# A decoder layer on one core: another written order for the first two row tiles' steps

## The chip, the cores and the metric

The kernel runs on one core of a Trainium2 chip. The core has a matrix engine (TensorE, PE in the profile, with PEld for its weight loads), a vector engine (VectorE, DVE), a scalar engine (ScalarE, ACT), a general engine (GpSimd, POOL) and an engine that here only issues transfers (SyncE, SP). Each works through a queue of its own in the order in which its instructions were put there; semaphores make one engine wait for another. The metric is the time of one execution in device microseconds (us), as the median of several runs. Lower is better.

## The reference

One layer of a decoder trunk over 1024 tokens behind 16 learned meta tokens, width 1024, all in float32:

```python
h = concat([meta, x])
u = rmsnorm(h, mix_norm_pre)
q, f_logit, i_in, g_out, v_pool, gate_a, gate_b = split(u @ w_in)
a = hgrn2(q, f_logit, i_in, g_out, ...)         # gated linear recurrence, 4 heads
p = multiscale_pool(v_pool, pool_proj, pool_scale)
z = sigmoid(gate_a) * (a @ w_branch_hgrn) + sigmoid(gate_b) * (p @ w_branch_pool)
h = h + rmsnorm(z @ w_out, mix_norm_post)
u = rmsnorm(h, ffn_norm_pre)
y = (gelu(causal_dwconv(u @ ffn_w_gate)) * (u @ ffn_w_up)) @ ffn_w_down
h = h + rmsnorm(y, ffn_norm_post)
return h[16:]
```

The change lies in the first microseconds: the norm `u` of the first rows and the columns `i_in` of the first product, `v = u @ w_in[:, 1024:1536]`.

## The kernel before

A float32 product is made from three products of a rounded type. Each operand is cut into a high part (rounded) and a low part (the rest, what the rounding left): high by high, high by low, low by high. On the weights' side a pair is `whi` and `wlo`; on the rows' side it is `uhi` and `ulo`. The rounding is done by ACT, the rest (a subtraction) by DVE. `mm3` (line 188) makes the three products at lines 190, 191 and 192: by `uhi` with `whi`, `uhi` with `wlo`, and `ulo` with `whi`.

Row tiles have 128 tokens. `vtiles` (line 458) lists nine, the 16 meta rows among them. The features (1024) are eight blocks of 128, called k. A product needs the rows with the features on the partitions, so each row tile is scaled by its norm, transposed by PE in 128 x 128 blocks (four into one PSUM bank, `pt`), and read out of PSUM twice, by ACT for `uhi` and by DVE for `ulo`. The weights of `v` arrive in four loads of 512 KB (`wiraw`), each with two k.

For the first two row tiles (number 0 and 1 in `vtiles`) the steps are written out one by one in a stage in which the order of ACT, DVE and PE is that of the text (`manual_schedule`, line 1033). The transfers were all issued ahead of it, on SP: row tile 0, weights 0, row tile 1, weights 1 to 3, and then the other rows. The step functions are these, with i the row tile, j a half of the row or a load of weights, k a feature block:

- `warm(n)` (line 501): n products of constants into a bank that nobody reads, which keep PE working while nothing else is there.
- `pe.transpose(gp, grow, ...)` and `gcol` (lines 1036 to 1038): the norm's gains are transposed and copied by DVE, so that k's gains stand along the partitions.
- `sq(i)`: ACT squares and sums row tile i, ACT takes the root, DVE the reciprocal.
- `scaled(i, j)`: DVE scales half j of row tile i into `un`.
- `turn(i, j)`: four PE transposes into the bank `pts[i, j]`, which then holds k = 4j to 4j+3.
- `hi_(i, k)` and `lo_(i, k)`: ACT multiplies by the gain and rounds into `uhi`; DVE multiplies and subtracts into `ulo`. Both read the bank.
- `wi_hi(j, part)` and `wi_lo(j, part)`: the same cut for load j of the weights, in halves (`ha`, `hb`, one k each) or whole.
- `mm_(i, k)`: the three products of row tile i and block k, summed in the bank `vb[i]`.

Behind these steps come `v_norm(2)` and `v_norm(3)` (norms of the next rows, on ACT and DVE), `v_feat` (their transposes, line 424), and the products of the other seven row tiles. The same stage runs on to the gates' first products. In later stages only PE's order is written out, and a planner, which works with modelled times when the kernel is built, sets the order of ACT, DVE, POOL and SP. The late stages use Strassen's form for the big products (lines 310 to 313), and the last product, with `w_down`, runs at lines 190 to 192 again.

Of the kernel before, what the change touches and what calls it, by code (L numbers as in the profile page):

```python
# [19 lines left out]
KD = D // P  # L20
# [49 lines left out]
def trunk_kernel(ctx: ExitStack, tc: tile.TileContext, x, meta_tokens, mix_norm_pre,  # L70
# [4 lines left out]
    act, dve, pool_e, pe = nc.scalar, nc.vector, nc.gpsimd, nc.tensor  # L75
# [20 lines left out]
    def nm(s):  # L96
        cnt[0] += 1
        return f"{s}_{cnt[0]}"
# [7 lines left out]
    def bank(name="ps"):  # L106
        return stage["ps", "p"].tile([P, 512], F32, tag="ps", name=nm(name))
# [11 lines left out]
    def small(shape, name, tag, bufs=4):  # L119
        return sm.tile(shape, F32, tag=tag, name=nm(name), bufs=bufs)  # L120

    def rr(a):
        return a.bitcast(F32)
# [377 lines left out]
    def warm(n):  # L501
        for _ in range(n):
            pe.matmul(junk_bank[:, :P], onesm, ident, start=True, stop=True)
# [12 lines left out]
    def v_mm(ps, t0, k):  # L516
        hi, lo = wi[k // 2]
        c = slice((k % 2) * 512, (k % 2) * 512 + 512)
        if t0 == 0:
            for n, b_ in ((2 * NM, hi), (NM, lo))[:: -1 if k else 1]:  # L520
                pe.matmul(ps[:n], um[:, k, :n], b_[:, c], start=(k == 0 and n > NM), stop=(k == KD - 1),
                          skip_group_check=True)
            return
        mm3(ps[:, :], (uhi[:, k, t0 : t0 + P], ulo[:, k, t0 : t0 + P]), (hi[:, c], lo[:, c]), k == 0, k == KD - 1)
# [506 lines left out]
    vb = [bank("pv") for _ in range(2)]  # L1031
    E = mybir.EngineType
    with tc.manual_schedule(engines={E.Activation, E.DVE, E.PE}):
        warm(8)
        gp = bank("pp")
        pe.transpose(gp[:, :KD], grow[:KD], ident[:KD, :KD])
        gcol = small([P, KD], "gcol", "gcol")
        dve.tensor_copy(gcol, gp[:, :KD])
        warm(6)
        wi += [tuple(wst.tile([P, 1024], F32R, tag=t, name=nm(t)) for t in ("whi", "wlo")) for _ in range(3)]  # L1040
        wi.append((slot(1024, F32R, "wihi"), slot(1024, F32R, "wilo")))
        pts, un_, rs_ = {}, {}, {}
# [1 line left out]
        def wi_hi(j, part=slice(0, 1024)):  # L1044
            act.copy(wi[j][0][:, part], raws[j][:, part])

        def wi_lo(j, part=slice(0, 1024)):
            dve.tensor_tensor(wi[j][1][:, part], raws[j][:, part], rr(wi[j][0][:, part]), ALU.subtract)

        def sq(i):  # L1050
            ssq = small([P, 1], "ssq", "nq")
            un_[i] = slot(D, name="un")
            act.activation(un_[i], rows_in[i], AF.Square, accum_out=ssq)
            rs_[i] = row_rstd(ssq, P, "n")

        def scaled(i, j):
            n = slice(j * 512, (j + 1) * 512)
            dve.tensor_scalar(un_[i][:, n], rows_in[i][:, n], rs_[i], None, ALU.mult)

        def turn(i, j):  # L1060
            pts[i, j] = bank("pt")
            for n in range(4):
                pe.transpose(pts[i, j][:, n * P : (n + 1) * P], un_[i][:, (4 * j + n) * P : (4 * j + n + 1) * P], ident)

        def u_at(i, k):
            t0 = vtiles[i][0]
            return (pts[i, k // 4][:, (k % 4) * P : (k % 4 + 1) * P], uhi[:, k, t0 : t0 + P], ulo[:, k, t0 : t0 + P])

        def hi_(i, *ks):
            for k in ks:  # L1070
                src, hi, lo = u_at(i, k)
                act.activation(hi, src, AF.Copy, scale=gcol[:, k : k + 1])

        def lo_(i, *ks):
            for k in ks:
                src, hi, lo = u_at(i, k)
                dve.scalar_tensor_tensor(lo, src, gcol[:, k : k + 1], rr(hi), ALU.mult, ALU.subtract)

        def mm_(i, *ks):
            for k in ks:  # L1080
                v_mm(vb[i], vtiles[i][0], k)

        ha, hb = slice(0, 512), slice(512, 1024)
        sq(0)
        scaled(0, 0)
        wi_hi(0, ha)
        wi_lo(0, ha)
        turn(0, 0)
        hi_(0, 0)
        lo_(0, 0)  # L1090
        wi_hi(0, hb)
        wi_lo(0, hb)
        hi_(0, 1)
        lo_(0, 1)
        mm_(0, 0, 1)
        scaled(0, 1)
        turn(0, 1)
        sq(1)
        hi_(0, 2, 3)
        wi_hi(1)  # L1100
        scaled(1, 0)
        turn(1, 0)
        lo_(0, 2)
        wi_lo(1, ha)
        scaled(1, 1)
        lo_(0, 3)
        wi_lo(1, hb)
        hi_(1, 0, 1)
        lo_(1, 0, 1)
        mm_(0, 2)  # L1110
        mm_(1, 0, 1)
        turn(1, 1)
        mm_(0, 3)
        hi_(0, 4, 5)
        lo_(0, 4, 5)
        hi_(1, 2, 3)
        wi_hi(2)
        lo_(1, 2, 3)
        wi_lo(2)
        mm_(1, 2, 3)  # L1120
        mm_(0, 4, 5)
        hi_(0, 6, 7)
        lo_(0, 6, 7)
        hi_(1, 4, 5)
        wi_hi(3)
        lo_(1, 4, 5)
        mm_(1, 4, 5)
        wi_lo(3)
        hi_(1, 6, 7)
        lo_(1, 6, 7)  # L1130
# [761 lines left out]
```

## Time and profile before

| | us |
|---|---|
| median of 3 runs | 1309.5 (1308.31 to 1310.21) |
| profiled execution, its own time | 1310.05 |
| span of that execution in the profile | 1308.3 |
| PE without work in the span (1308.3 less 1291.9 busy) | 16.4 |
| first useful product of the two tiles starts | 9.48 |
| transposes behind their last product start | 24.31 |

Times of rows in the trace are us from the span's start. A row of the timeline gives start, duration, engine, line, operation, what is written from what, the shape, and how many like instructions were merged (x); in brackets stands the idle time of the engine ahead of it and what ended that. A row of the waits gives who waited for whom: total, times, longest. A row of the windows gives the stretch, its length, the busy time of PE, PEld, DVE, ACT and POOL with their instructions, the granted clock of PE, the share of the DMA engines and GB/s. A PE row's duration runs to the modelled end of a product; products overlap, and what counts is the distance of their starts.

### The profile page before, as it was taken

What the parts mean: (1) busy time and instruction counts of PE and PEld (TensorE: products, weight loads), DVE (VectorE), ACT (ScalarE), POOL (GpSimd) and SP (SyncE); (2) the same over time, 40 slices, a digit from 0 to 9 for tenths busy, and PEclk for the clock granted to TensorE, in tenths of its full rate; (3) what the DMA queues carried; (4) which work ended last, traced back from release to release, by engine and by line L of the source; (5) the groups of instructions that cost most, each with busy time, mean ns of one, the idle gap of its engine ahead of it and who ended that gap; (6) DMA issues with size and microseconds to landing.
All of it is one profiled execution on the core that took longest, in us unless ns stands there. A gap on an engine that the chain in (4) does not pass through costs nothing.

```text
span 1308.3 us, 21993 instructions
## 1 busy us (share of the span) xinstructions
PE 1291.9 (99%) x8651; PEld 1140.8 (87%) x8651; DVE 965.3 (74%) x1311; ACT 527.2 (40%) x918; POOL 356.1 (27%) x308
## 2 busy tenths in 40 slices
PE   8999999999999999999999999999999999999998
PEld 7799899999999899978898888888888888888887
DVE  6768965454776877765588999888898985455758
ACT  6554433332244546235563222322322232444443
POOL 3015333130000000150045655553755552000000
PEclk9999999999999999999999999999999999999999
DMA  8135542325524767776777787568777799666644
GB/s 277 42 106 164 194 158 102 122 89 153 170 67 144 231 236 238 281 224 242 242 257 249 192 222 176 172 181 207 167 180 169 154 247 294 209 225 226 227 173 161
DMA packets 143817, 247.62 MB, mean 189 GB/s; under 512 B 11008, under 2 KB 75180, under 8 KB 143714
## 3 DMA queue, kind: packets, MB, share of 16 engines
q1 hardware_dynamic: 127026, 213.42, 48.7%
q0 software_dynamic: 12064, 24.38, 11.3%
q10 hardware_dynamic: 4624, 8.41, 1.7%
q8 instruction: 68, 1.11, 0.4%
q14 instruction: 35, 0.29, 0.1%
HBM read 174.12 MB, written 95.09 MB: 206 GB/s over the span
## 4 chain that ended last, share of the span: by engine, by line
PE 95%; DVE 1%; ACT 1%; DMA 1%; issue 0%; POOL 0%; DVEq 0%; ACTq 0%; SPq 0%; POOLq 0%
PE P L310 17%; PE P L311 17%; PE P L313 17%; PE pd L190 5%; PE pd L191 5%; PE pd L192 5%; PE pm L190 2%; PE pm L192 2%; PE pm L191 2%; PE ppv L210 1%; PE ppv L214 1%; PE ppv L211 1%; PE pba L210 1%; PE pba L211 1%; PE pg L210 1%; PE pv L192 1%
## 5 line engine op out<-in xcount | busy, mean ns | idle before, releaser
L311 PE MATMUL P<-v,whi 128*128 128x512 f32 (+2 forms) x408 | 140.7, 353 | 0.0
L310 PE MATMUL P<-v,whi 128*128 128x512 f32 (+2 forms) x408 | 140.7, 352 | 0.0
L313 PE MATMUL P<-v,wlo 128*128 128x512 f32 (+2 forms) x424 | 135.1, 349 | 0.0
L281 POOL TENSOR_TENSOR swa<-wraw,wraw 128x512 f32<-128x512 f32 x32 | 48.9, 1530 | 188.0 <-DMA wraw<-in_w_in_dram 77.3
L255 ACT CAST whi<-wraw 128x512 fp32r<-128x512 f32 x90 | 53.1, 618 | 101.5 <-PE P L311 86.9
L1602 DVE TENSOR_TENSOR rot<-wraw,rot 128x1024 fp32r<-128x1024 f32 x31 | 38.0, 1225 | 72.2 <-ACT rot L1601 72.2
L310 PEld LDWEIGHTS P<-v,whi 128*128 128x128 f32 x408 | 76.7, 188 | 10.4
L311 PEld LDWEIGHTS P<-v,whi 128*128 128x128 f32 x408 | 76.6, 188 | 10.2
L313 PEld LDWEIGHTS P<-v,wlo 128*128 128x128 f32 x424 | 74.0, 188 | 10.8
L192 PE MATMUL pd<-rot 128*128 128x512 f32 x274 | 82.5, 388 | 0.0
L191 PE MATMUL pd<-rot 128*128 128x512 f32 x274 | 82.5, 388 | 0.0
L190 PE MATMUL pd<-rot 128*128 128x512 f32 x274 | 81.9, 388 | 0.1
L256 DVE TENSOR_TENSOR wlo<-wraw,whi 128x512 fp32r<-128x512 f32 x86 | 74.5, 889 | 2.7 <-ACT whi L255 2.7
L255 ACT CAST whi<-swa 128x512 fp32r<-128x512 f32 x64 | 38.2, 619 | 91.9 <-PE P L311 81.2
L256 DVE TENSOR_TENSOR wlo<-swb,whi 128x512 fp32r<-128x512 f32 x64 | 67.9, 1068 | 9.0 <-ACT whi L255 8.7
L1601 ACT CAST rot<-wraw 128x1024 fp32r<-128x1024 f32 x31 | 32.7, 1054 | 90.8 <-PE pd L192 89.4
L310 PE MATMUL P<-uhi,whi 128*128 128x258 f32 (+2 forms) x240 | 68.6, 303 | 0.0
L311 PE MATMUL P<-ulo,whi 128*128 128x258 f32 (+2 forms) x240 | 68.4, 303 | 0.0
L255 ACT CAST whi<-swb 128x512 fp32r<-128x512 f32 x64 | 38.1, 618 | 69.3 <-PE P L311 61.0
L310 PE MATMUL P<-t2h,whi 128*128 128x258 f32 (+2 forms) x228 | 65.3, 304 | 0.3 <-DVE sg L869 0.3
L310 PE MATMUL P<-t4h,whi 128*128 128x258 f32 (+2 forms) x228 | 65.5, 304 | 0.0
L311 PE MATMUL P<-t4l,whi 128*128 128x258 f32 (+2 forms) x228 | 65.4, 304 | 0.0
(399 smaller groups left out, 3849.3 us busy)
## 6 DMA issues: line engine op xcount, KB each, us to landing
wraw<-in_w_in_dram SPq DMA_DIRECT2D x36, 512.0 KB, 4.5
yt<-ysum SPq DMA_DIRECT2D x33, 512.0 KB, 5.3
wraw<-in_ffn_w_gate_dram SPq DMA_DIRECT2D x26, 512.0 KB, 7.1
wraw<-in_ffn_w_up_dram SPq DMA_DIRECT2D x22, 512.0 KB, 6.8
wsum<-in_ffn_w_down_dram SPq DMA_DIRECT2D x22, 512.0 KB, 8.2
wraw<-in_w_out_dram SPq DMA_DIRECT2D x18, 512.0 KB, 5.1
ysum<-ys SPq DMA_DIRECT2D x11, 768.0 KB, 6.4
sa<-sscr SPq DMA_DIRECT2D x16, 513.0 KB, 7.1
```

The source lines that it names most:

```text
L190: pe.matmul(ps, ahi, bhi, start=first, stop=False)
L191: pe.matmul(ps, ahi, blo, start=False, stop=False)
L192: pe.matmul(ps, alo, bhi, start=False, stop=last)
L210: pe.matmul(ps[:, :n], whi[:, k, :], xhi, start=(k == 0), stop=False)
L255: act.copy(hi, src)
L256: (pool_e if 4 <= i < 2 * self.early else dve).tensor_tensor(lo, src, rr(hi), ALU.subtract)
L281: pool_e.tensor_tensor(s1, a21, a22, ALU.add)
L310: pe.matmul(d, whi[:, k, :], xh[:, c : c + w], start=(k == 0 and onto is None), stop=False, **go)
L311: pe.matmul(d, whi[:, k, :], xl[:, c : c + w], start=False, stop=False, **go)
L313: pe.matmul(x[:, o : o + w], wlo[:, k, :], xh[:, c : c + w], start=False, stop=(k == 3), **go)
L1601: act.copy(hi, src)
L1602: dve.tensor_tensor(lo, src, rr(hi), ALU.subtract)
```

## The change

The steps of row tiles 0 and 1 are written in another order; none is added or left out, but for the dummies.

- Ahead of the gains' transpose stand 11 calls of `warm` instead of 8, behind it 2 instead of 6.
- The copy `gcol` moves behind `scaled(0, 0)` on DVE.
- Load 0 of the weights is rounded in both halves by ACT, and its rests are made by DVE, ahead of any `hi_` and `lo_`. `hi_` of k = 0 and 1 then stand together, and so do their `lo_`.
- `scaled(1, 0)` and `turn(1, 0)` come ahead of `hi_(0, 2)` and `lo_(0, 2)` instead of behind the `hi_`.
- Load 1 of the weights is rounded in halves, each between the cuts of k = 2 and k = 3, and `mm_(0, 2)` and `mm_(0, 3)` follow their half.
- `scaled(1, 1)` moves behind the cuts and products of tile 1's first two blocks.
- For the later blocks the cuts and products come tile by tile, with the same pairs.

```diff
-        warm(8)
+        warm(11)
         gp = bank("pp")
         pe.transpose(gp[:, :KD], grow[:KD], ident[:KD, :KD])
         gcol = small([P, KD], "gcol", "gcol")
-        dve.tensor_copy(gcol, gp[:, :KD])
-        warm(6)
+        warm(2)
...
         sq(0)
         scaled(0, 0)
+        dve.tensor_copy(gcol, gp[:, :KD])
+        turn(0, 0)
         wi_hi(0, ha)
+        wi_hi(0, hb)
         wi_lo(0, ha)
-        turn(0, 0)
-        hi_(0, 0)
-        lo_(0, 0)
-        wi_hi(0, hb)
         wi_lo(0, hb)
-        hi_(0, 1)
-        lo_(0, 1)
+        hi_(0, 0, 1)
+        lo_(0, 0, 1)
         mm_(0, 0, 1)
         scaled(0, 1)
         turn(0, 1)
         sq(1)
-        hi_(0, 2, 3)
-        wi_hi(1)
         scaled(1, 0)
         turn(1, 0)
+        hi_(0, 2)
         lo_(0, 2)
+        wi_hi(1, ha)
         wi_lo(1, ha)
-        scaled(1, 1)
+        mm_(0, 2)
+        hi_(0, 3)
         lo_(0, 3)
+        wi_hi(1, hb)
         wi_lo(1, hb)
+        mm_(0, 3)
         hi_(1, 0, 1)
         lo_(1, 0, 1)
-        mm_(0, 2)
         mm_(1, 0, 1)
+        scaled(1, 1)
         turn(1, 1)
-        mm_(0, 3)
+        hi_(1, 2, 3)
+        lo_(1, 2, 3)
+        mm_(1, 2, 3)
         hi_(0, 4, 5)
+        wi_hi(2)
         lo_(0, 4, 5)
-        hi_(1, 2, 3)
-        wi_hi(2)
-        lo_(1, 2, 3)
         wi_lo(2)
-        mm_(1, 2, 3)
         mm_(0, 4, 5)
+        hi_(1, 4, 5)
+        lo_(1, 4, 5)
         hi_(0, 6, 7)
+        wi_hi(3)
+        mm_(1, 4, 5)
         lo_(0, 6, 7)
-        hi_(1, 4, 5)
-        wi_hi(3)
-        lo_(1, 4, 5)
-        mm_(1, 4, 5)
         wi_lo(3)
         hi_(1, 6, 7)
         lo_(1, 6, 7)
```

## The prediction

> **What bounds the kernel now.** I read the page first: its busy line and its chain of work.
>
> ```profile
> PE 1291.9 (99%) x8651; PEld 1140.8 (87%) x8651; DVE 965.3 (74%) x1311; ACT 527.2 (40%) x918; POOL 356.1 (27%) x308
> ...
> PE 95%; DVE 1%; ACT 1%; DMA 1%; issue 0%; POOL 0%; DVEq 0%; ACTq 0%; SPq 0%; POOLq 0%
> ```
>
> TensorE (PE) is busy in 1291.9 of 1308.3 us, and the chain that ended last is 95% PE. So an edit pays only what it takes out of PE's 16.4 us of idleness, or what products it removes. The diff touches only work up to the last product of the first two row tiles. I therefore asked for the busy times of that stretch and the list of waits in it.
>
> ```profile
> 9.48:24.30 14.82, 13.84 (x60) 10.14 (x61) 12.85 (x31) 11.51 (x28) 1.72 (x3) 1.00 1.01 354
> ...
> DVE ulo L1077 <- ACT uhi L1072: 2.2, 2, 2.0
> ...
> ACT uhi L1072 <- DVE ulo L1077: 1.6, 2, 1.3
> ...
> PEld pv L191 <- DVE wlo L1048: 0.8, 2, 0.5
> PEld pv L192 <- DVE ulo L1077: 0.8, 1, 0.8
> ```
>
> Here no engine is the bound: PE, DVE and ACT hand work round. The timeline tells the rhythm (start, duration, engine, line).
>
> ```profile
> 5.73 0.60 ACT L1045 CAST whi<-wiraw 128x512 fp32r<-128x512 f32 x1
> ...
> 5.75 0.27 PE L1036 MATMUL pp<-ident,grow 8*128 8x8 f32 x1
> 5.95 2.64 PE L503 MATMUL pj<-ident,onesm 128*128 128x128 f32 x12
> ...
> 6.33 0.49 DVE L1058 TENSOR_SCALAR un<-row,rstd 128x512 f32<-128x512 f32 x1
> ...
> 8.43 0.60 PE L1063 MATMUL pt<-ident,un 128*128 128x128 f32 x4
> 9.06 0.37 ACT L1072 ACTIVATE uhi<-pt,gcol 128x128 fp32r<-128x128 f32 x1 [2.74 <-PE pt L1063]
> ...
> 9.48 0.50 PE L190 MATMUL pv<-whi,uhi 128*128 128x512 f32 x1 [0.46 <-ACT uhi L1072]
> ...
> 10.12 1.05 ACT L1053 ACTIVATE un<-row 128x1024 f32<-128x1024 f32 x1
> ...
> 10.84 0.48 DVE L1058 TENSOR_SCALAR un<-row,rstd 128x512 f32<-128x512 f32 x1
> ...
> 11.38 0.66 PE L1063 MATMUL pt<-ident,un 128*128 128x128 f32 x4
> ...
> 11.81 0.49 DVE L1058 TENSOR_SCALAR un<-row,rstd 128x512 f32<-128x512 f32 x1
> 11.99 1.04 ACT L1045 CAST whi<-wiraw 128x1024 fp32r<-128x1024 f32 x1
> ...
> 12.45 0.63 PE L1063 MATMUL pt<-ident,un 128*128 128x128 f32 x4 [0.42 <-DVE un L1058]
> ...
> 14.33 0.68 DVE L1048 TENSOR_TENSOR wlo<-wiraw,whi 128x512 fp32r<-128x512 f32 x1
> ...
> 14.93 1.12 DVE L1077 SCALAR_TENSOR_TENSOR ulo<-pt,gcol,uhi 128x128 fp32r<-128x128 f32 x4
> ...
> 15.33 0.50 PE L192 MATMUL pv<-whi,ulo 128*128 128x512 f32 x1 [0.32 <-DVE ulo L1077]
> ...
> 15.56 0.63 ACT L1072 ACTIVATE uhi<-pt,gcol 128x128 fp32r<-128x128 f32 x2 [1.30 <-DVE ulo L1077]
> ...
> 16.73 0.48 PE L190 MATMUL pv<-whi,uhi 128*128 128x512 f32 x1
> ...
> 17.16 1.23 DVE L1048 TENSOR_TENSOR wlo<-wiraw,whi 128x1024 fp32r<-128x1024 f32 x1 [0.33 <-ACT whi L1045]
> ...
> 19.97 1.06 ACT L408 ACTIVATE un<-row 128x1024 f32<-128x1024 f32 x1
> ...
> 23.20 1.60 DVE L413 SCALAR_TENSOR_TENSOR un<-row,rstd,g 128x512 f32<-128x512 f32 x2
> ...
> 24.31 1.91 PE L424 MATMUL pt<-ident,un 128*128 128x128 f32 x16
> ```
>
> The two tiles need 48 products. From 16.73 to 24.31, 33 products less one start-up of 0.09 run without a gap, so one costs 0.227. 48 of them are 10.9 us, and three groups of four transposes inside cost about 0.45 each, 1.3. The stretch from 9.48 to 24.31 lasts 14.8. Some 2.6 us are gaps and restarts, the most that a better order can win there. Nearly all lie before 16.73.
>
> **The change, part by part.** (1) *Dummy products.* Each warm call is two PE instructions (six calls gave x12). The rows below give their pace.
>
> ```profile
> 2.04 3.78 PE L503 MATMUL pj<-ident,onesm 128*128 128x128 f32 x16 [2.04 <-POOL ident masks.py:199]
> ...
> 5.40 0.42 PE L503 MATMUL pj<-ident,onesm 128*128 128x128 f32 x1
> ...
> L503 PE MATMUL pj<-ident,onesm x28: 274/421/582, 2.0 to 8.3; 128*128 128x128 f32 x28
> ```
>
> Sixteen start between 2.04 and 5.40: 0.37 for the first, then 0.213 each. The last take 274 ns instead of 421, so the array doubled its pace near 8.2. The call total falls from 14 to 13, which is two instructions, at 0.11 to 0.213 each: 0.2 to 0.4. The gain transpose moves from 5.75 to 7.03 (six instructions by 0.213), four dummies end near 8.2, and the first row transposes start at 8.2 instead of 8.43. Their input (un, 6.82) is ready under either order. I take 0.2.
>
> The Trainium skill (TensorE: Matmul & The Clock Gate, Part 1) says that the array starts at half clock, and gets the full clock only after a busy window of about 3.4 us whose phase runs free. It speaks against thinning dummies. By that rule the window may close as late as 2.04 + 2 x 3.41 = 8.87, an estimate from that page; the trace's doubling near 8.2 agrees. The new busy stretch (dummies, then four transposes) runs to 8.8 at full clock and beyond 9 at half, so the rule leaves my sum alone.
>
> (2) *gcol's copy* goes behind the first scaling on DVE and waits there for the transpose, to about 7.5. Behind it stand the two rests of the first weights, 0.68 each: ready at 8.9. The earliest reader is the product at 9.6, so this costs nothing. If it had no cover, one rest would delay PE by 0.68 at most.
>
> (3) *Weights 0 rounded whole and first.* ACT does its second half at 6.3 to 6.9, in its 2.74 us of idleness, instead of between the first two roundings of u. That takes 0.6 off ACT's path before sq(1). But the two roundings now stand together before their two rests. ACT's and DVE's reads of one transposed bank exclude each other as written (ACT at 15.56 waited 1.30 for DVE's rests of that bank), so the first rest waits for the second rounding. Call T the end of the transposes' wait: 9.06 before, 8.85 now. The roundings take T to T+0.62 and the rests T+0.65 to T+1.26. The six products start at T+0.42, the third waits until T+1.05, and the last slot ends at T+1.96, that is 10.81. Before it was 11.38. Running gain: 0.57.
>
> (4) *Scaling and squares.* scaled(0,1) follows the rests, 10.05 to 10.5, ready for transposes at 10.81. sq(1) starts at T+0.52 = 9.37 instead of 10.12. Its input row must be there. If loads land in the order issued (row 0, weights 0, row 1, weights 1; 0.524 MB each), these rows decide:
>
> ```profile
> 0.00:7.50 7.50, 5.46 (x24) 5.22 (x25) 1.38 (x5) 3.44 (x6) 6.86 (x33) 1.00 0.72 253
> 0.00:9.30 9.30, 6.99 (x33) 6.50 (x33) 1.38 (x5) 3.67 (x7) 7.11 (x34) 1.00 0.78 278
> ```
>
> By 7.5 us 253 x 7.5 = 1.90 MB have moved, against 1.57 MB for row 0, weights 0 and row 1. By 9.3 it is 2.59 MB, against 2.10 with weights 1. If they land only when before used them (10.12, 11.99), 0.75 of the gain is lost: the lower bound. From sq(1) to scaled(1,0)'s end took 10.12 to 12.30, so now 9.37 to 11.55. The transposes of tile 1 start at 11.65 (12.45 before): PE idles 0.4 here.
>
> (5) *Weights 1 in halves.* DVE runs lo(0,2) at 11.5, rest a at 11.75 to 12.45, lo(0,3) (its rounding waits for lo(0,2), the bank again) at 12.35, and rest b at 12.75 to 13.45. PE takes mm(0,2) at 12.1, waits for rest a until 12.5, takes mm(0,3) at 13.05, and waits for rest b until 13.5. Ends at 14.05. Each of the two waits is at most 0.45 with its restart, where before the single longest were 0.5 (wlo) and 0.8 (ulo).
>
> (6) *Tile 1 and the rest.* From 14.05 to the end PE has 6 products to 15.45, transposes to 15.8, then 30 products and one restart (6.9). Is everything ready? lo(1,0,1) 14.0 against 14.5; scaled(1,1) 14.4 against 15.45; lo(1,2,3) 15.3 against 16.3; rest of weights 2 17.4 against 17.5 (the tightest); rest of weights 3 19.6 against 20.2; lo(1,6,7) 20.15 against 21.8. So PE ends at 22.7 instead of 24.31: 1.6 us. The gain is thus 0.2 from dummies, 0.35 from the first six products, and the rest from shorter waits on rests.
>
> (7) *Behind it.* Norm 2 on ACT starts at 18.7 (19.97), so un(2) is ready at 21.85, un(3) at 23.55, and their transposes need them at 22.7 and 24.0. All is shifted alike. The diff issues nothing to SP or POOL and moves nothing past their queues. PE's later waits are on DVE and ACT, which move with PE.
>
> Bounds: 0.8 (late loads, or 0.05 more at each of a dozen hand-overs) and 1.9 (rests not excluded by the bank). I take 1.6. The profiled execution took 1310.05, 1.75 more than its span: the sum is 1310.05 - 1.6 = 1308.45. It lies 0.55 above the median of 1309.5, so the forecast for a median is **1307.9 us**, or -0.12%.
>
> **The rivals.** *The gain is eaten at once*: by (4)'s lower bound, or because rest 2, with 0.1 to spare, becomes late. For it: DVE is busy 12.85 of 14.82. Against: loads are ahead. 1308.7.
>
> *Order later changes.* Behind the hand-written stage, ACT's and DVE's order comes from a planner that works with its own times, and one late place is fragile.
>
> ```profile
> PE po L797 <- DVE st L779: 2.0, 1, 2.0
> PE pbb L210 <- DVE uhi L848: 1.7, 1, 1.7
> ...
> 435.00:440.00 5.00, 3.03 (x12) 2.66 (x13) 5.00 (x10) 3.65 (x7) 0.00 (x0) 0.82 1.08 334
> ...
> 495.00:500.00 5.00, 2.96 (x24) 2.68 (x23) 3.10 (x6) 1.63 (x2) 0.00 (x0) 0.97 0.84 310
> 500.00:505.00 5.00, 5.00 (x24) 5.00 (x24) 4.89 (x7) 4.69 (x6) 0.00 (x0) 0.69 0.48 151
> ```
>
> A 2.0 us stall of PE near 499 drags the granted clock down behind it: 0.03 x 5 + 0.31 x 5 = 1.7 us of clock lost. So one such stall is worth 3.7. *Faster*: this stall dissolves, 1304.2. *Slower*: one more arises in the head stage (360 to 505 us), when the planner puts a weight rest that waits for its load ahead of a DVE step that PE needs. It decides from about 1.7 us of idle PE, where the second row shows the clock falling. 1307.9 + 3.7 = 1311.6. For either: the change shifts the planner's times. Against: it shifts all engines nearly alike.
>
> *The clock comes one window later*, with twelve transposes and seven products at half pace: 12 x 0.11 (the pitch of the four at 8.43) + 7 x 0.227 = 2.9 at most, 1310.8. The busy stretch of (1) speaks against it.
>
> **How the numbers follow.** Forecast 0.59; eaten 0.15; stall gone 0.12; stall added 0.11; late clock 0.03. About 0.2% (2.6 us) is what a measurement here can tell from no change. Faster by more: the dissolved stall and a 0.04 tail of the forecast with smaller shifts, 0.16. Slower by more: the added stall and 0.01 else, 0.12. Same: 0.72. The forecast's own range, from its bounds and the 1.9 us between the runs shown, is 1306.4 to 1309.4. The whole range runs into both stall cases, 1304.6 to 1311.2, and leaves about 0.12 out.
>
> **What would show it.** The first row transposes at 8.2; the first product at about 9.3; tile 1's transposes at 11.65; waits of PE on wlo of 0.2 each; the transposes of L424 at 22.7. Wrong would be: L424 above 23.5 (step 4, 5 or 6), products at twice 0.227 behind 8.8 (step 1), or L424 early and the span not shorter (step 7: then look at the waits on st and uhi and the clock near 440 and 500).

## The result, and the profile after

| | before | after |
|---|---|---|
| median, us (22 runs each) | 1308.26 (1307.11 to 1310.76) | 1306.72 (1304.68 to 1309.53) |
| ratio, 95% interval | | 0.9986 (0.998 to 0.9993) |
| profiled execution, its own time | 1310.05 | 1304.68 |
| its span | 1308.3 | 1303.0 |
| first row transposes start | 8.43 | 7.67 |
| transposes behind the two tiles' last product start | 24.31 | 22.20 |
| between these two | 15.88 | 14.53 |

The change wins 1.54 us by the medians, 0.12%; the ratio on record, with an interval that leaves out 1, is 0.9986. The forecast was 1.6 us or 0.12% from a median of 1309.5 that three runs had given; over 22 runs before's median is lower by 1.2.

First the busy line of the page of after, and the windows row of the stage, from its first useful product to the transposes of L424.

```profile
PE 1287.3 (99%) x8649; PEld 1136.9 (87%) x8649; DVE 966.8 (74%) x1311; ACT 527.2 (40%) x919; POOL 353.7 (27%) x308
```

```profile
8.72:22.20 13.48, 13.26 (x61) 10.05 (x61) 12.00 (x30) 11.07 (x28) 0.00 (x0) 1.00 0.97 353
```

This stretch lasted 14.82 us before, so it is 1.34 shorter. PE stands without work for 0.22 us of it instead of 0.98. DVE's busy time in it fell by 0.85 and ACT's by 0.44, because a rest and a rounding of weights 0 that lay inside it now lie ahead of it. The timeline of after shows where.

```profile
5.82 1.14 ACT L1044 CAST whi<-wiraw 128x512 fp32r<-128x512 f32 x2
...
7.12 0.71 PE L503 MATMUL pj<-ident,onesm 128*128 128x128 f32 x4
...
7.31 1.29 DVE L1047 TENSOR_TENSOR wlo<-wiraw,whi 128x512 fp32r<-128x512 f32 x2
...
7.67 0.60 PE L1062 MATMUL pt<-ident,un 128*128 128x128 f32 x4
8.30 0.63 ACT L1071 ACTIVATE uhi<-pt,gcol 128x128 fp32r<-128x128 f32 x2 [1.35 <-PE pt L1062]
...
8.72 0.50 PE L190 MATMUL pv<-whi,uhi 128*128 128x512 f32 x1 [0.46 <-ACT uhi L1071]
...
8.82 1.06 ACT L1052 ACTIVATE un<-row 128x1024 f32<-128x1024 f32 x1
...
8.96 0.61 DVE L1076 SCALAR_TENSOR_TENSOR ulo<-pt,gcol,uhi 128x128 fp32r<-128x128 f32 x2 [0.36 <-ACT uhi L1071]
...
10.40 0.60 PE L1062 MATMUL pt<-ident,un 128*128 128x128 f32 x4
...
11.16 0.63 PE L1062 MATMUL pt<-ident,un 128*128 128x128 f32 x4 [0.16 <-ACT whi L1044]
...
11.93 0.50 PE L191 MATMUL pv<-wlo,uhi 128*128 128x512 f32 x1
...
12.96 0.50 PE L191 MATMUL pv<-wlo,uhi 128*128 128x512 f32 x1
...
13.46 1.14 ACT L1071 ACTIVATE uhi<-pt,gcol 128x128 fp32r<-128x128 f32 x4 [0.75 <-DVE ulo L1076]
...
22.20 1.91 PE L424 MATMUL pt<-ident,un 128*128 128x128 f32 x16
```

Both halves of weights 0 are rounded in one stretch from 5.82 and their rests are made from 7.31, while PE runs dummies and the first transposes. Counted from the start of the first rounding of u (9.06 before, 8.30 now), tile 0's second transposes come at 2.10 us instead of 2.32, tile 1's first at 2.86 instead of 3.39, and L424 at 13.90 instead of 15.25. That is 1.35 us of the stage. The two reads of one bank exclude each other as before: DVE's first rest waits 0.36 for the second rounding, and ACT at 13.46 waits 0.75 for DVE.

The two profiled spans lie 5.3 us apart, far more than the medians. 2.11 of that is there at L424. Most of the rest comes from the head stage, as the granted clock shows there (the rows of before stand in the prediction: 0.82 from 435 to 440, and 0.97 and 0.69 from 495 to 505).

```profile
435.00:440.00 5.00, 4.28 (x54) 3.71 (x57) 5.00 (x11) 2.25 (x4) 0.00 (x0) 1.00 0.99 330
...
495.00:500.00 5.00, 5.00 (x34) 5.00 (x33) 5.00 (x7) 4.92 (x7) 0.00 (x0) 1.00 0.55 179
```

Before had two stretches of about 3.4 us at half clock there, after none. Whether that belongs to the change is a question for the experiments: POOL's and SP's instructions did not change their order, nor ACT's behind the first two row tiles, and in the stages left to the planner a single DVE instruction did (line 681 of one head, now behind line 729).

### The profile page after: what moved, and what is told of

The parts are those of the page before. It is cut to its first block, busy times and chain, and to the rows that moved or that the text cites. A ratio compares the mean times of both kernels' runs of the same rounds, so it can differ in the third digit from the quotient of the medians.

```text
span 1303.0 us, 21990 instructions
## 1 busy us (share of the span) xinstructions
PE 1287.3 (99%) x8649; PEld 1136.9 (87%) x8649; DVE 966.8 (74%) x1311; ACT 527.2 (40%) x919; POOL 353.7 (27%) x308
## 4 chain that ended last, share of the span: by engine, by line
PE 96%; ACT 2%; DVE 1%; issue 1%; DMA 0%; POOL 0%; DVEq 0%; ACTq 0%; POOLq 0%
PE P L310 17%; PE P L311 17%; PE P L313 17%; PE pd L190 5%; PE pd L191 5%; PE pd L192 5%; PE pm L190 2%; PE pm L192 2%; PE pm L191 2%; PE ppv L210 1%; PE ppv L214 1%; PE ppv L211 1%; PE pba L210 1%; PE pba L211 1%; PE pg L210 1%; PE pv L191 1%
```

## The experiments

My theory: the written order makes the gain in the stage, the dummies add 0.2 us, and the whole passes to the end; half-clock stretches in the head stage are a matter of the single run. The main rivals: the dummies make the gain, or the half-clock stretches do. In the table "stage" is the time from the first row transposes to L424, "half" the number of half-clock stretches in the head stage of the profiled run, and "ratio" the one on record to the runs of before on the same chip (it is near the quotient of the two medians, but not the same).

| kernel | first transposes | L424 | stage | half | median | before | ratio (95%) |
|---|---|---|---|---|---|---|---|
| e1 order only | 7.22 | 21.80 | 14.58 | 1 | 1306.38 | 1308.18 | 0.9985 (0.9977 to 0.9994) |
| e2 dummies only | 7.22 | 23.12 | 15.90 | 1 | 1308.23 | 1308.18 | 0.9997 (0.9988 to 1.0006) |
| e3 24 more dummy calls | 12.88 | 27.43 | 14.55 | 1 | 1313.51 | 1308.18 | 1.004 (1.0027 to 1.0052) |
| e4 square of tile 1 earlier | 7.64 | 24.08 | 16.44 | 1 | 1307.72 | 1308.18 | 0.9992 (0.9983 to 1.0001) |
| e5 few dummies | 6.47 | 21.56 | 15.09 | 0 | 1307.42 | 1307.75 | 0.9995 (0.9986 to 1.0004) |
| e6 weights 0 as before | 7.78 | 22.89 | 15.11 | 0 | 1307.18 | 1307.75 | 0.9991 (0.9982 to 1.0) |
| e7 wide dummies | 13.62 | 28.17 | 14.55 | 1 | 1312.35 | 1307.75 | 1.0032 (1.0019 to 1.0044) |
| e8 a bank for k = 0 | 7.17 | 21.72 | 14.55 | 1 | 1305.92 | 1307.75 | 0.998 (0.997 to 0.9989) |
| e9 after, again | 7.63 | 22.21 | 14.58 | 1 | 1306.07 | 1308.31 | 0.9985 (0.9976 to 0.9993) |
| e10 e8 again | 7.09 | 21.56 | 14.47 | 2 | 1305.66 | 1308.31 | 0.9984 (0.9975 to 0.9993) |
| e11 e5, second look | 6.64 | 21.90 | 15.26 | 0 | 1306.25 (one run) | 1308.31 | |
| e12 before, second look | 7.39 | 23.28 | 15.89 | 1 | 1307.15 (one run) | 1308.31 | |

### The order alone, the dummies alone (e1, e2)

```diff
# e1, from after
-        warm(11)
+        warm(8)
...
-        warm(2)
+        warm(6)
# e2, from before
-        warm(8)
+        warm(11)
...
-        dve.tensor_copy(gcol, gp[:, :KD])
-        warm(6)
+        warm(2)
...
         scaled(0, 0)
+        dve.tensor_copy(gcol, gp[:, :KD])
```

> The kernel after with the dummies of before (8 calls ahead of the gains' transpose, 6 behind it). Theory (the order of the steps makes the gain, and it is carried to the end): from the first row transposes to the transposes of L424 it takes about 14.5 us, as in the kernel after (22.20 - 7.67 = 14.53), against 15.88 before (24.31 - 8.43); whole time 1.2 us under before. Rival (the gain is a matter of half-clock windows later in the run): the stage is 1.3 us shorter, but the whole time follows the number of half-clock windows in the run and isn't reliably under before. Rival (dummies make the gain): 15.9 us, time as before.

> The kernel before with the dummies of after (11 and 2 calls, the gains' copy behind the first scaling). Theory: from the first row transposes to L424 about 15.9 us as before; only their start moves, by 0.2 to 0.4 us at an equal moment of the clock's rise; whole time 0.2 to 0.4 under before, not to be told from it. Rival (dummies make the gain): 1.5 us under before.

The two ends of the stage in the timeline of e1, then of e2, and its start in e12, which is the kernel before:

```profile
7.22 0.60 PE L1062 MATMUL pt<-ident,un 128*128 128x128 f32 x4
...
21.80 1.36 PE L424 MATMUL pt<-ident,un 128*128 128x128 f32 x11
```

```profile
7.22 0.60 PE L1063 MATMUL pt<-ident,un 128*128 128x128 f32 x4
...
23.12 1.14 PE L424 MATMUL pt<-ident,un 128*128 128x128 f32 x9
```

```profile
7.39 0.60 PE L1063 MATMUL pt<-ident,un 128*128 128x128 f32 x4
```

Both start their row transposes at the same moment, and the order brings L424 1.32 us ahead. The whole time follows: the order alone has the ratio of the full change, and the dummies alone can't be told from before. Each of the two profiles has one half-clock stretch, so that the rival of those stretches falls for this pair. e2 and e12 show the dummies' share: in both the starts of the dummies go from 0.21 to 0.11 us apart at the same moment, between 5.8 and 6.2, and the row transposes start at 7.22 and 7.39. That is 0.17 us for two instructions fewer.

### The first weights in the order of before (e6)

```diff
# from after
         wi_hi(0, ha)
-        wi_hi(0, hb)
         wi_lo(0, ha)
+        hi_(0, 0); lo_(0, 0)
+        wi_hi(0, hb)
         wi_lo(0, hb)
-        hi_(0, 0, 1)
-        lo_(0, 0, 1)
+        hi_(0, 1); lo_(0, 1)
```

> The kernel after with the cuts of weights 0 and of u's first two blocks in the order of before (rounding and rest of half a, cut of k = 0, then half b, cut of k = 1). Theory (weights 0 first takes 0.6 us off ACT's path to tile 1's square, which PE waits for): from the first row transposes to L424 15.0 to 15.1 us against 14.5 of the kernel after. Rival (the pairing of the cuts gives back what the earlier weights win): 14.5 us.

From the timeline of e6, the first transposes, the square of tile 1 and L424:

```profile
7.78 0.60 PE L1062 MATMUL pt<-ident,un 128*128 128x128 f32 x4
...
9.47 1.05 ACT L1052 ACTIVATE un<-row 128x1024 f32<-128x1024 f32 x1
...
22.89 0.38 PE L424 MATMUL pt<-ident,un 128*128 128x128 f32 x2
```

The stage takes 15.11 us, as the theory had it. The square starts 1.05 us behind the first rounding (8.42) instead of 0.52, and L424 comes 14.47 behind it instead of 13.90. So of the stage's 1.35 us some 0.57 come from the first weights. The rest, by difference, comes from the later reordering; which of its moves gives how much was not tested.

### The square still earlier (e4)

```diff
# from after
         wi_lo(0, hb)
+        sq(1)
         hi_(0, 0, 1)
...
         turn(0, 1)
-        sq(1)
```

> The kernel after with the square and the norm of row tile 1 ahead of the first two roundings of u, where ACT is idle for 1.35 us. Theory (behind the first six products PE waits on the path through tile 1's square): that path leaves; tile 1's transposes follow tile 0's second four without the 0.3 us gap, the waits for the rests of weights 1 shrink; from the first row transposes to L424 13.8 us against 14.5; whole time about 2.2 under before. Rival (the rests on DVE are the bound behind the first products, whatever the square does): 14.3 to 14.5 us.

Both theories missed. The timeline of e4, and the windows row of the granted clock there:

```profile
8.01 1.06 ACT L1052 ACTIVATE un<-row 128x1024 f32<-128x1024 f32 x1 [1.15 <-DMA row<-in_x_dram]
...
9.79 0.50 PE L190 MATMUL pv<-whi,uhi 128*128 128x512 f32 x1 [1.55 <-ACT uhi L1071]
```

```profile
6.80:10.20 3.40, 1.85 (x13) 1.34 (x11) 1.71 (x5) 2.02 (x6) 0.48 (x4) 1.00 1.02 380
10.30:13.60 3.30, 3.30 (x12) 2.67 (x12) 2.94 (x8) 1.75 (x4) 0.00 (x0) 0.50 1.03 366
```

ACT, which works in order, waited for the row until 8.01; the roundings of u stood behind the square, and the first product came at 9.79 instead of 8.72. PE was then busy for only 1.85 of 3.40 us, and for the next 3.4 us the clock was granted by half. The row lands at about 8.0, not near 7.5 as the prediction's bytes had it; in after the square asks for it at 8.82 and does not wait.

### Few dummies (e5, and a second look, e11)

```diff
# from after
-        warm(11)
+        warm(6)
...
-        warm(2)
+        warm(0)
```

> The kernel after with 6 calls of dummies ahead of the gains' transpose and none behind it, so that PE idles from about 5 us until the first scaled row at 6.5 us. Theory (the array's clock rises only after a stretch of about 3.4 us without a gap, which the dummies give): the first row transposes start at 6.6 us, but the first products run at half pace, 0.43 us each instead of 0.23; L424 at 22.2 to 23.5, whole time as after or up to 1.3 us over it. Rival (the dummies only hold the stage up): L424 at 21.1 us, whole time 1.1 us under the kernel after.

> A second look at the kernel of e5. Theory (the clock rises at the end of a window of 3.4 us that lies on a grid of the run's own and is busy; with a gap in PE's work from 5 to 6.5 us a run whose grid doesn't fit rises late): the clock rises only behind 9 us, the first products start 0.43 us apart, and L424 comes at 22.5 to 23.5. If the grid fits, it rises at 5.5 again and L424 comes at 21.6 as in the first look. Rival (the gap never matters): 21.6 in any case.

From the timeline and the waits of e5:

```profile
8.12 1.06 ACT L1052 ACTIVATE un<-row 128x1024 f32<-128x1024 f32 x1 [0.35 <-DMA row<-in_x_dram]
...
21.56 0.27 PE L424 MATMUL pt<-ident,un 128*128 128x128 f32 x1
...
432.63 0.62 PE L704 MATMUL sl<-q,k 128*32 128x16 f32 x51 [1.31 <-issue]
433.49 0.42 PE L210 MATMUL pbb<-uhi,whi 128*128 128x342 f32 x1 [0.23 <-DVE uhi L848]
...
PE po L797 <- DVE st L779: 2.3, 2, 1.7
```

And of e11:

```profile
8.78 0.63 PE L191 MATMUL pv<-wlo,uhi 128*128 128x512 f32 x1
9.21 0.63 PE L192 MATMUL pv<-whi,ulo 128*128 128x512 f32 x1
9.63 0.63 PE L190 MATMUL pv<-whi,uhi 128*128 128x512 f32 x1
...
21.90 0.27 PE L424 MATMUL pt<-ident,un 128*128 128x128 f32 x1
```

The rows of after for the end of e5's:

```profile
434.19 0.42 PE L210 MATMUL pbb<-uhi,whi 128*128 128x342 f32 x1 [1.75 <-DVE uhi L848]
...
PE po L797 <- DVE st L779: 1.4, 1, 1.4
```

In the first look the array ran at full pace from the first product on; in the second the products start 0.43 apart until past 10 us. So half pace, which the theory of e5 foresaw, was missing in the first look and came in the second: when the clock rises is a matter of the run. The theory's price was wrong: L424 comes only 0.34 later, because at full pace ACT waits for tile 1's row (0.35, until 8.12 in e5), and at half pace its square starts only 0.17 later, at 8.29.

L424 is even ahead of after's, but the whole time isn't: e5 is 0.33 under before by the medians, after 1.54. In both looks PE stands 1.3 us inside the head stage's short products at L704. "issue" is a gap without a releaser in the profile. But here this gap costs nothing: the next product waits for DVE for 0.23 us instead of 1.75, and comes as far behind L424 in e5 as in after (411.93 and 411.99). What is lost lies further on. PE waits for `st` for 2.3 us in two waits where after has 1.4 in one; why it does so is not shown.

### Is a shift of the stage carried to the end? (e3, e7)

```diff
# e3, from after
-        warm(2)
+        warm(26)
# e7, from after
-        warm(11)
+        warm(5)
...
-        warm(2)
+        [pe.matmul(junk_bank, onesm, ident.rearrange("p (o c) -> p o c", o=1).to_broadcast([P, 4, P]), start=True, stop=True) for _ in range(8)]
```

> The kernel after with 24 more calls of dummies (48 instructions) behind the gains' transpose. Theory (what the stage wins or loses is carried whole to the end): L424 is 48 x 0.11 = 5.2 us later than in the kernel after, less the little that ACT and DVE run ahead in that time (their waits of PE in the stage go, some 1 us): 26.3 to 27.4; the whole time rises by the same 4.1 to 5.2 us, to about 2.6 to 3.7 over before. Rival (later stages have slack that takes a shift up): L424 as late, but the whole time rises by under half of it.

> The kernel after with as many PE instructions, but of the 13 calls of dummies 8 are four times as wide and stand behind the gains' transpose: a start that is 4 to 5 us later without one more instruction. Theory (a shift of the stage is carried whole, and what e3_late_start took beyond its shift came from its 48 more instructions): the whole time is over the kernel after by as much as L424 is later than 22.2 us, within 0.6 us. Rival (a late start costs the later stages 1.6 us more, because loads and PE then meet otherwise): over it by that shift and 1.6 us.

e3's L424 was late as foreseen (27.43, by 5.23 over after), but the whole time rose by 5.33 over before, hence by 6.9 over after: 1.6 too much. Its timeline has a gap of PE at L704 too, which no profile with as many instructions as after has, and here the products behind it stay late:

```profile
438.90 0.42 PE L210 MATMUL pbb<-uhi,whi 128*128 128x342 f32 x1 [1.75 <-DVE uhi L848]
...
451.31 0.44 PE L704 MATMUL sl<-q,k 128*32 128x16 f32 x32 [1.19 <-issue]
```

Ahead of that gap the shift is whole: the product at 438.90 comes 411.5 us behind L424, against 412.0 in after and 411.6 in e1. e7 has a late start too, but not one PE instruction more:

```profile
13.62 0.60 PE L1062 MATMUL pt<-ident,un 128*128 128x128 f32 x4
...
28.17 0.38 PE L424 MATMUL pt<-ident,un 128*128 128x128 f32 x2
```

It is late by 5.97 us at L424, its list of waits has no such gap, and its median is 4.60 over before: 6.1 over after (4.60 + 1.54). So a shift of the stage is carried whole as far as five runs can tell. Their intervals (2.5 to 5.8 us over before for e7, 3.5 to 6.8 for e3) rule out the rival that half of it is taken up (at most 1.5 and 1.1 over before), but not an error of a microsecond, so that by the times alone e3's 1.6 are not clear of noise.

### A bank of its own for k = 0 (e8, e10)

```diff
# from after, in turn and u_at
-                pe.transpose(pts[i, j][:, n * P : (n + 1) * P], ...
+                pe.transpose(junk_bank[:, 384:] if (i, j, n) == (0, 0, 0) else pts[i, j][:, n * P : (n + 1) * P], ...
...
-            return (pts[i, k // 4][:, ...
+            return (junk_bank[:, 384:] if (i, k) == (0, 0) else pts[i, k // 4][:, ...
```

> The kernel after with tile 0's block k = 0 transposed into the bank of the dummies, so that its rest and the rounding of k = 1 read different banks. Theory (two reads of one bank by ACT and DVE exclude each other in the order written; and behind the first six products PE waits for tile 1's square): the first rest starts 0.03 us behind its own rounding, some 0.27 us earlier; the third product follows the second after about 0.25 instead of 0.31 us and tile 0's second transposes come 0.2 us earlier, but tile 1's first transposes stay at 3.5 us behind the first ones, and from these to L424 it takes 14.3 to 14.5 us. Rival (the first rest is late for another reason, such as gcol or the rests of the weights ahead of it): it starts as late as in the kernel after, 0.66 us behind the first rounding's start.

> The kernel of e8 once more beside the kernel after. Theory (PE waits for tile 1's square, so a bank of its own for k = 0 wins nothing at the end of the stage): from the first row transposes to L424 14.5 us as in e9, whole time the same within 0.5 us. Rival (it wins the 0.4 us by which its second transposes come earlier): 14.1 us, 0.4 under e9.

The timeline of e8:

```profile
7.81 0.37 ACT L1071 ACTIVATE uhi<-pt,gcol 128x128 fp32r<-128x128 f32 x1
...
8.03 0.34 DVE L1076 SCALAR_TENSOR_TENSOR ulo<-pj,gcol,uhi 128x128 fp32r<-128x128 f32 x1
...
9.46 0.60 PE L1062 MATMUL pt<-ident,un 128*128 128x128 f32 x4
...
10.64 0.63 PE L1062 MATMUL pt<-ident,un 128*128 128x128 f32 x4 [0.58 <-ACT whi L1044]
```

The first rest starts at 8.03 while the second rounding runs (7.81 to 8.18), as soon as DVE is done with the weights' rests: with two banks the exclusion is gone. Tile 0's second transposes come 2.29 us behind the first instead of 2.73. Tile 1's first come 3.47 behind, against 3.49: PE only waits longer for them. The stage is as long as in after (14.55 and 14.47), and beside it on one chip the whole time is 0.4 us lower (1305.66 against 1306.07), with intervals that lie on each other. Its ratios of 0.998 and 0.9984 put it clearly ahead of before; ahead of after it wasn't shown to be.

### The run's own share (e9, e12)

Both are the unchanged kernels once more.

> The kernel after once more, beside e10. Theory (the moment at which the array's clock rises, and the half-clock windows in the head stage, are a matter of the run; the stage's length is not): from the first row transposes to L424 again 14.5 us, though the clock's rise falls anywhere from 5.4 to 8.9 us and the number of later half-clock windows may be 0, 1 or 2; whole time 1.3 to 1.8 under before. Rival (the after kernel has fewer half-clock windows of its own): again none in the head stage.

> A second look at the kernel before. Theory: from the first row transposes to L424 15.9 us again; the clock's rise, 8.15 in the first look, falls elsewhere, and so do the half-clock windows of the head stage. Rival (8.15 and two later half-clock windows belong to this kernel): the same again.

The stage is the run-independent part: 14.53 and 14.58 for after, 15.88 and 15.89 for before. The start isn't: before's first transposes came at 8.43 in one run and 7.39 in the other. Nor are the half-clock stretches, as the windows of the second looks at after and then at before show:

```profile
495.00:500.00 5.00, 4.72 (x22) 4.73 (x23) 4.30 (x6) 3.83 (x6) 0.00 (x0) 0.67 0.36 109
```

```profile
435.00:440.00 5.00, 4.50 (x18) 4.25 (x19) 5.00 (x12) 2.18 (x4) 0.00 (x0) 0.66 1.07 362
```

This time after has one and before has one. Their number was 0, 1 or 2 in the fourteen profiles. From L424 to the end of the span it took 1280.8 (after) and 1281.4 (e6) with none, 1281.6 to 1284.4 with one, 1284.0 and 1284.2 with two; e5 and e11, with none but the longer waits told of above, took 1282.1 and 1282.6.

Fourteen profiles are few, but every run has its granted clock on record. Its mean is 0.9976 over 33 runs of after (the first 22 and e9's) and 0.9974 over the 75 runs of before beside the experiments, a difference worth some 0.3 us. Among runs with the same listed clock (0.996, 0.997, 0.998 or 0.999) after's mean time is lower by 0.7, 1.6, 1.8 and 1.8 us. So the gain is not one of fewer half-clock stretches, and the first profiles' 5.3 us were 1.5 of change and the rest the draw of two runs.

## Why the prediction was right

**Which work bounds.** Right. PE was short of ready work in the stage. Behind it PE has waits for DVE of 1.4 to 2.0 us, but they move along with a shift and take nothing of it up: e7's is carried to the end.

**Step 1, dummies, 0.2 us.** Right: 0.17 between e2 and e12, at the same rise of the clock. The moment of 8.43 for before's start was one run's, and with it all of the forecast's moments: the first transposes came at 7.67 instead of 8.2 and L424 at 22.20 instead of 22.7, both half a microsecond early. The length of the stage does not hang on this.

**Step 2, gcol's copy, nothing.** Right: the copy was done at 7.4 and the rests of weights 0 at 8.6, ahead of the product that asks for them at 9.06.

**Step 3, first weights, 0.35 besides the dummies.** Its path was right, its size at that place too large: the first six products with their waits won 0.22 (2.10 against 2.32), not 0.36. The sum let the product behind the wait follow after 0.227; it followed after 0.34 (9.37 to 9.71). What e6 takes away is 0.57, because the earlier square pays again behind them.

**Step 4, the square.** Right in effect: 0.52 behind the first rounding, as foreseen, and tile 1's transposes at 2.86 behind it where the sum had 2.80. The landing of its row was 0.5 us or more too early in the estimate from bytes; e4 fell over this. That the change did not was slack that the sum had not worked out.

**Steps 5 and 6, weights 1 and the rest.** Right: L424 at 13.90 behind the first rounding, in the sum 22.7 - 8.85 = 13.85. The waits for the two rests of weights 1 are there: the products behind them come 3.63 and 4.66 behind the first rounding (11.93 and 12.96), in the sum 3.65 and 4.65.

**Step 7, behind it.** Right for the order (e1 has the ratio of the whole change). The two rivals with a stall of the head stage were no other state of the kernel: the stall at st stayed (1.4 us in after's first profile, 2.0 in its longest in the second), and with it the half-clock stretch, which some runs have and some don't. So a stall of about 1.7 us does not by itself bring the clock down, as the prediction read it: in after PE waits 1.75 us until 434.19, and the clock stays at 1.00. The rivals "eaten" and "late clock" didn't occur; what they would look like, e4 and e11 show.

**The clock's rule.** The rule of the Trainium skill weighed in step 1 (TensorE: Matmul & The Clock Gate, Part 1) held where dummies ran without a gap: the pace doubled before the first useful product in every such profile. With a gap from 5 to 6.5 us it did so in one of two looks.

**The forecast.** 1.6 us was forecast and 1.54 measured, with an interval of 0.9 to 2.6; that the two agree to 0.06 is luck. What the runs bear out more closely is the sum for the stage: 1.40 from the first rounding on (15.25 less 13.85) against 1.35, and 0.2 against 0.17 for the dummies. The absolute forecast, 1307.9, lies 1.2 over the measured 1306.72, because the median of three that it started from was high by as much. "The same within 0.2%" had 0.72 of the chance, and so it came.

## What to carry to other kernels

In a stage where three engines hand work round, follow the chain from engine to engine and ask which hand-over PE waits for last: earlier work pays only on that chain (the first weights), and elsewhere it only lengthens the wait (the bank of its own). Ahead of moving a step up on an engine that works in order, see when its input lands: a step that waits holds everything behind it. And compare stages, not spans, where a microsecond matters: the stage repeated to 0.05 us while the spans of one kernel lay 3 us apart.

## What the runs showed of the hardware

- **The clock can fall although PE works half of the time.** In e4 PE was busy for 1.85 of 3.40 us and the next 3.3 us were granted at 0.50. A stall of 1.4 to 2.0 us in the head stage has the same effect in some runs and none in others.
- **With another number of PE instructions ahead, PE can stand still far behind.** With 74 dummy instructions (e3) or 12 (e5, e11) PE stood for 1.2 to 1.3 us inside the short products of L704, with no releaser in the profile; with 26 or 28 it did so in none of the other eleven profiles. In e3 the products behind stayed late, in e5 and e11 the next wait was shorter by as much. The cause was not tested.
- **Loads in a row land later than their bytes suggest.** The third of 0.524 MB was waited for until 8.01 us in e4 and 8.12 in e5, while in e4 1.96 MB had moved by 7.5, where three such loads are 1.57.
